# Neighbourhood attention: scores as one float32 product in four 64x64 tiles, 24 key columns per query half, bias tables from the host, value products joined over halves

## The chip, the cores and the metric

The kernel runs on one core of one Trainium2 chip. The metric is the device time of one execution in microseconds (us); lower is better. A core has TensorE (PE; its weight loads are listed apart as PEld), VectorE (DVE), ScalarE (ACT), GpSimd (POOL) and SyncE (SP), which here issues nearly all DMAs. Each engine takes its instructions in the order in which the program gives them.

## The reference

One layer over 2048 tokens of width 1024, which form a grid of 32 rows by 64 columns:

```python
h = rmsnorm(x, g)                                  # x (1, 2048, 1024), g = norm_0
q, k, v, gate = jnp.split(h @ w_in, 4, axis=-1)    # w_in (1024, 4096); 16 heads of 64
# per head; query (r, c); keys in 8 rows from clip(r - 4, 0, 24), 16 columns from clip(c - 8, 0, 48)
s = (q . k) / 8 + rpb[head, key_row - r + 7, key_col - c + 15]
o = softmax(s over those 128 keys) @ v
x = x + (o * silu(gate)) @ w_out                   # w_out (1024, 1024)
out = rmsnorm(x, norm_f)
```

All is float32. The learned bias `rpb` has 15 x 31 numbers per head.

## The kernel before

**Projections.** In the first half of the span (`stage_one`, `stage_two`) TensorE makes most of q, k, v and the gate. A product of float32 precision is there three products of values rounded to fewer bits (`F32R`): high x high, high x low, low x high. ScalarE copies the high half of an operand, VectorE subtracts it from the whole to get the low half. Results go to DRAM by `give`: q as it is, the gate after tanh, k split once more into a high and a low half (`hi`, `lo`, lines 370 to 375), which are stored apart.

**Attention.** It runs over 32 steps, one per pair of heads `p` and block of 8 query rows `T`, in the order `order`: T = 0 for all 8 pairs, then T = 1 and 2 for each pair, then T = 3 for all. Block T sees 11, 15, 15 or 12 key rows (`KEY_ROWS`). The 64 grid columns fall into four blocks C of 16; a block's queries (8 rows x 16 columns = 128, ordered as two halves of 8 columns each) see 24, 32, 32 or 24 key columns (`KEY_COLS`).

- `scores` (line 1025): for each C and each of the two heads `s` three F32R products, q's high and low half (split per step by `split_q`, which also scales by 1/8) against k's. The heads lie on partitions 0 to 63 and 64 to 127, so a product takes 64 rows of the array and all 128 columns. VectorE then adds the table `EM` and takes the minimum of the negated sum (line 1046); ScalarE takes the exponential with its sum (1052).
- Tables: the bias of a pair is loaded as padded rows (`load_e`) and POOL adds a mask to it per column kind (`bias`, line 1004); for T = 3 the finished table is loaded in six pieces (`load_last`).
- `normalise` (1055): a reciprocal on VectorE, then a multiplication per tile on POOL; in the second call of a step ScalarE does two of the four.
- `turns` (1087): 44 transposes of 64 queries each by TensorE into six PSUM banks; ScalarE and VectorE copy these to `pta` (1097).
- `values` (1126): per C, for each strip of 8 key columns, one float32 product per head, over 128 queries where both halves see the strip and over 64 where one does: 28 products per step. The heads take the two halves of the array's columns. VectorE multiplies by the gate (1149), and the result goes to DRAM for the output projection.

**Order of the work.** The main loop (1441 to 1487) writes it out by hand. In cycle m, `begin` queues loads; `feed` issues what is left of the projections, then of the output projection, about 24 matmuls per cycle in cycles 1 to 24 and more after; `consume` and `split_rows` put weight and activation splits between; then come `turns(m - 1)`, the two `scores` of step m and the `values` of step m - 1. `store(key, lag, f)` and `due` put a load or store on SyncE when the clock, which counts issued matmuls, has passed the lag. There are 8 PSUM banks, handed round in turn to projections, transposes, scores and values.

Of the kernel before, what the change touches and what calls it, by code (L numbers as in the profile page):

```python
# [10 lines left out]
F32 = mybir.dt.float32  # L11
# [13 lines left out]
RPB_ROWS, RPB_W = 26, 32  # L25
# [9 lines left out]
KEY_COLS = [(0, 24), (8, 40), (24, 56), (40, 64)]  # L35
# [4 lines left out]
MASK_N = [[(u1 - u0) * (v1 - v0) for v0, v1 in TYPE_COLS] for u0, u1 in TYPE_ROWS]  # L40
MASK_ALL = sum(sum(n) for n in MASK_N[:2])
LAST_ALL = sum(MASK_N[2])
# [3 lines left out]
def mask_table():  # L46
    out = []
    for t, (u0, u1) in enumerate(TYPE_ROWS):
        T = (0, 1, 3)[t]
        for c, (v0, v1) in enumerate(TYPE_COLS):  # L50
            C = (0, 1, 3)[c]
            half, qr, col, strip, kr, kc = np.ogrid[:2, T * 8:T * 8 + 8, :8, :(v1 - v0) // 8, T * 8 + u0:T * 8 + u1, :8]
            qc = C * 16 + half * 8 + col
            kc = C * 16 + v0 + strip * 8 + kc
# [3 lines left out]
            out.append(np.where(ok, 0.0, NEG).astype(np.float32).reshape(128, -1))  # L58
    return np.concatenate(out, axis=1)


def strips(C):
    out = []
    for s in range(KEY_COLS[C][0] // 8, KEY_COLS[C][1] // 8):
        halves = [h for h in range(2) if abs(2 * C + h - s) <= 1]
        out.append((s, s - KEY_COLS[C][0] // 8, halves[0] * 64, len(halves) * 64))
    return out
# [3 lines left out]
def build(ctx, tc, x, xr, xt, wg, rpb, last, w_out, n0, nf, masks, out):  # L71
# [4 lines left out]
    k_hi = [dram.tile([128, S], F32, name=f"k_hi{p}") for p in range(NP)]  # L76
    k_lo = [dram.tile([128, S], F32, name=f"k_lo{p}") for p in range(NP)]
# [12 lines left out]
    kp = pool("kp", 4)  # L90
# [14 lines left out]
    mp = pool("mp", 6)  # L105
# [41 lines left out]
    MK = []  # L147

    def load_masks():
        MK.append(mkp([128, MASK_ALL], BF16, "mk"))  # L150
        nc.sync.dma_start(MK[0], masks)


# [16 lines left out]
    def use_item(it):  # L170
# [6 lines left out]
        elif kind == "w":  # L177
# [12 lines left out]
            nc.scalar.activation(h, t, AF.Copy)  # L190
            nc.vector.tensor_tensor(l, t, h.bitcast(F32), OP.subtract)
# [102 lines left out]
    quiet = [False]  # L294

# [56 lines left out]
    def give(kind, hp, c, t, bank_=False):  # L352
# [11 lines left out]
        if kind == "q":  # L364
            if bank_:
                t = ev([128, 512], F32, "q")
                nc.scalar.activation(to(t), at, AF.Copy)
            store(("q", hp, c), 12, lambda: nc.sync.dma_start(qd[hp][:, s], t))
            return
# [39 lines left out]
    def seven_products(us, c0, X1, also):  # L409
# [11 lines left out]
        def form(n, P):  # L421
            src = A[n, uses[P][0]]
            F[n, P] = t = wp([128, 2, 512], F32R, "f")
            nc.scalar.activation(t[:, 0], src, AF.Copy)  # L424
            nc.vector.tensor_tensor(t[:, 1], src, t[:, 0].bitcast(F32), OP.subtract)  # L425
# [143 lines left out]
    def place_of(slot_):  # L569
        return slot_[0]([128, slot_[1]], F32R, "t")[:, :512] if isinstance(slot_, tuple) else slot_  # L570
# [6 lines left out]
    def stage_one():  # L577
        us = [("k", j) for j in range(4)] + [(k, j) for j in range(4) for k in "qg"]
        X1 = {f: [(xs([128, 512], F32R, "h"), xs([128, 512], F32R, "l")) for _ in range(4)]
              for f in ("B12", "B11", "B21", "B22")}  # L580
        spot = mkp([128, 3, 512], F32, "spot")
        land = {f: [p([128, n], F32, "land")[:, :512] for _ in range(4)]
                for f, p, n in (("x12", kp, 960), ("x22", xp, 512), ("x11", vh, 512))}
        sixth = sixths()
        land["x21"] = [spot[:, k] for k in range(3)] + [lp([128, 512], F32, "land")]
        slots = [(mp, 512)] * 6 + [(qp, 512)] * 2 + [(sp, 512)] * 2 + sixth[:2] + [(vh, 512)] * 4
        slots += sixth[2:] + [(kp, 960)] * 4
# [4 lines left out]
        def split(f, t, k, scale=None):  # L592
            if f == "T1":
                X1.setdefault(f, []).append((xs([128, 512], F32R, "h"), xs([128, 512], F32R, "l")))
            elif f[0] == "T":
                X1.setdefault(f, []).append((place_of(slots.pop(0)), place_of(slots.pop(0))))
# [4 lines left out]
        def load_rows(*hs):  # L601
            for t, j in hs:
                rows_in[t, j] = mp([128, 512], F32, "row")
                nc.sync.dma_start(rows_in[t, j], xr[t * 128:t * 128 + 128, 512 * j:512 * j + 512])

        def square_rows(*hs):
            for t, j in hs:
                square(t, j, rows_in.pop((t, j)))
# [192 lines left out]
    def stage_two():  # L801
# [3 lines left out]
        for k in range(4):  # L805
            load_x(2, "x22", k, x22[k])
        slots = {"T2": [(mp, 512)] * 4 + [(kp, 960)] * 4,
                 "T3": [(sp, 512)] * 2 + sixth[:5] + [(lp, 512)],
                 "T4": [(vh, 512)] * 4 + [(mp, 512)] * 2 + [sixth[5], (qp, 512)]}

        def also(n, i):
            if n == 0:
                if i == 0:
                    load_ahead()
                    load_e(0, 0, xp)[0]()
                elif i == 1:
                    load_e(0, 0, xp)[1]()
                    load_masks()
# [4 lines left out]
                if i in (4, 5):  # L823
                    bias(0, 0, i - 4)
                if i == 3:
                    for f in load_k(0, 0) + [load_q(0, 0)]:
                        f()
                if i == 5:
                    split_q(0, 0)
# [45 lines left out]
        def form(f, x, *ks):  # L875
            def g():
                for k in ks:
                    h, l = (place_of(a) for a in slots[f][2 * k:2 * k + 2])
# [55 lines left out]
    KT, VT, QT, EM, SG, E = {}, {}, {}, {}, {}, {}  # L934
# [9 lines left out]
    def width(C):  # L944
        return KEY_COLS[C][1] - KEY_COLS[C][0]

    def load_k(p, T):
        r0, r1 = KEY_ROWS[T]
        n = (r1 - r0) * GW
        must(*[("k", p, c) for c in range(r0 // 8, (r1 + 7) // 8)])  # L950
        KT[p, T] = []

        def keys(src):
            t = kp([128, 960], F32R, "kt")
            KT[p, T].append(t.rearrange("p (r c) -> p r c", c=GW))
            nc.sync.dma_start(t[:, :n].bitcast(F32), src[p][:, r0 * GW:r1 * GW])

        return [lambda: keys(k_hi), lambda: keys(k_lo)]

    def load_q(p, T):  # L960
        must(("q", p, T))

        def queries():
            QT[p, T] = t = lp([128, 512], F32, "qr")
# [3 lines left out]

    def split_q(p, T):
        t = QT[p, T]  # L970
        QT[p, T] = h, l = qp([128, 512], F32R, "qh"), qp([128, 512], F32R, "ql")
        split_to(h, l, t, HD ** -0.5)
# [13 lines left out]
    def load_e(p, ty, pool_=None):  # L986
        r0, r1 = (4, 15) if ty == 0 else (0, 15)

        def rows(s):
            t = (pool_ or ep)([128, 512], F32, "e")[:, :480]  # L990
            E[p, s] = t.rearrange("p (u v) -> p u v", v=32)
            nc.sync.dma_start(t[:, r0 * 32:r1 * 32], rpb[2 * p + s][:, r0 * 32:r1 * 32])

        return [lambda: rows(0), lambda: rows(1)]

    def bias(p, ty, cty):
        m0 = sum(sum(n) for n in MASK_N[:ty]) + sum(MASK_N[ty][:cty])
        (u0, u1), (v0, v1) = TYPE_ROWS[ty], TYPE_COLS[cty]
        n = MASK_N[ty][cty]
        sh = lambda a: a.rearrange("p (s u v) -> p s u v", u=u1 - u0, v=8)  # L1000
        for s in range(2):
            t = mp([128, 512], F32, "em")[:, :n]
# [537 lines left out]
```

## Time and profile before

| | |
|---|---|
| median of 3 runs | 1068.65 us (1068.24 to 1069.79) |
| span of the profiled execution | 1068.2 us, 0.4 below that median |
| busy: TensorE, VectorE, ScalarE, POOL | 1052.0, 739.8, 551.3, 261.9 us |
| score products, L1038 | 768 records, 550 to 999 us |
| value products, L1143 | 1792 records, 571 to 1013 us |
| transposes, L1121 | 1408 records, 566 to 1009 us |
| bias and mask on POOL, L1004 | 94 operations, 92.6 us |
| normalising on POOL and ScalarE, L1064 and L1062 | 192 and 64 operations |
| DMA | 206.53 MB |

A line of a group names the kernel's line, the engine and the operation, what is written and read, the shape, the count, the busy time and the mean length of one. Matmuls are pipelined: the length of one includes its way through the array, so the distance from start to start tells what it costs. In the order of time, records that follow each other and belong to one group are merged: start, length of the whole, count. A shape of 64\*128 means 64 rows and 128 columns of the array.

### The profile page before, as it was taken

The numbers are of one execution on the slowest core, as the hardware profiler recorded it, in microseconds if no ns is written. First come the engines' busy times: TensorE is split into PE (matmuls) and PEld (weight loads), VectorE is DVE, ScalarE is ACT, GpSimd is POOL, SyncE is SP. The second block draws the span as 40 slices with busy tenths as digits, with TensorE's granted clock in tenths as the row PEclk, the third lists the DMA queues.
The fourth block names the chain that finished last, engine by engine and source line by source line (L and its number), as shares of the span: only waits on it lengthen the run. The fifth ranks groups of instructions, "written<-read, shape, count | busy, mean of one in ns | idle before, by whom it ended". The sixth has DMA issues, their size and how long they took to land.

```text
span 1068.2 us, 20961 instructions
## 1 busy us (share of the span) xinstructions
PE 1052.0 (98%) x7596; PEld 876.8 (82%) x7596; DVE 739.8 (69%) x1608; ACT 551.3 (52%) x1285; POOL 261.9 (25%) x328
## 2 busy tenths in 40 slices
PE   9999999999999999999999999999998999999997
PEld 6888888887888888888888888888877888888886
DVE  5476888768897635566568677767777786667644
ACT  7645344333334334333347767778686765556422
POOL 0000322312311000000017775555445421212100
PEclk9999999999999999999999999999999999999999
DMA  9633665344645333524298789877986688787352
GB/s 320 212 99 108 197 205 178 124 134 140 176 129 150 116 89 92 173 90 169 85 317 265 230 244 302 266 237 237 295 271 214 209 285 294 223 262 252 105 158 79
DMA packets 129472, 206.53 MB, mean 193 GB/s; under 512 B 11800, under 2 KB 56088, under 8 KB 129368
## 3 DMA queue, kind: packets, MB, share of 16 engines
q1 hardware_dynamic: 128936, 204.79, 60.7%
q8 instruction: 60, 0.98, 0.4%
q14 instruction: 44, 0.36, 0.1%
q10 hardware_dynamic: 432, 0.40, 0.1%
HBM read 146.42 MB, written 58.72 MB: 192 GB/s over the span
## 4 chain that ended last, share of the span: by engine, by line
PE 86%; DVE 6%; DMA 2%; ACT 2%; issue 2%; POOL 1%; SPq 0%; DVEq 0%; ACTq 0%; POOLq 0%
PE pp L442 31%; PE pv L566 16%; PE s L1038 7%; PE o L1143 6%; PE po L1354 5%; PE po L1352 5%; PE po L1350 5%; PE ph L1121 3%; PE pp L390 3%; PE pp L388 3%; PE pp L386 3%; DVE x L1046 1%; DVE f L425 1%; DVE wol L196 1%; ACT x L1052 1%
## 5 line engine op out<-in xcount | busy, mean ns | idle before, releaser
L442 PE MATMUL pp<-h,f 128*128 128x512 f32 x608 | 196.7, 389 | 0.0
L1064 POOL TENSOR_SCALAR x<-x,st 128x480 f32<-128x480 f32 (+5 forms) x192 | 110.6, 593 | 261.9 <-DVE st L1057 240.4
L1052 ACT ACTIVATE x<-x,st 128x360 f32<-128x360 f32 (+5 forms) x256 | 151.2, 592 | 29.4 <-DVE st L1046 29.3
L1004 POOL TENSOR_TENSOR em<-e,mk 128x264 f32<-128x264 f32 (+3 forms) x94 | 92.6, 1019 | 211.1 <-DMA mk<-in_masks_dram 210.3
L442 PEld LDWEIGHTS pp<-h,f 128*128 128x128 f32 x608 | 114.1, 188 | 23.7
L442 PE MATMUL pp<-t,f 128*128 128x512 f32 x506 | 128.5, 390 | 0.3
L462 POOL TENSOR_TENSOR tmp<-tmp,rb 128x512 f32<-128x512 f32 x36 | 58.6, 1630 | 269.7 <-DVE tmp L460 210.3
L1046 DVE CUSTOM_DVE_ANT_0 x<-s,em 128x360 f32<-128x360 f32 (+5 forms) x256 | 123.4, 536 | 1.0 <-PE s L1038 1.0
L442 PE MATMUL pp<-l,f 128*128 128x512 f32 x304 | 118.3, 389 | 0.0
L442 PEld LDWEIGHTS pp<-t,f 128*128 128x128 f32 x506 | 94.8, 188 | 20.8 <-DVE u L455 1.1
L1354 PE MATMUL po<-wol,gh 128*128 128x512 f32 x252 | 99.3, 394 | 0.0
L1352 PE MATMUL po<-woh,gl 128*128 128x512 f32 x252 | 98.9, 392 | 0.3 <-DVE gl L1208 0.3
L1350 PE MATMUL po<-woh,gh 128*128 128x512 f32 x252 | 98.4, 391 | 0.0
L1038 PE MATMUL s<-kt,qh 64*128 64x480 f32 (+5 forms) x512 | 86.0, 382 | 7.6 <-issue 2.3
L566 PE MATMUL pv<-wh,h 128*128 128x512 f32 x256 | 88.8, 392 | 0.5 <-ACT h L527 0.5
L425 DVE TENSOR_TENSOR f<-raw,f 128x512 fp32r<-128x512 f32 x95 | 73.2, 771 | 22.4 <-ACT f L424 22.4
L566 PE MATMUL pv<-wl,h 128*128 128x512 f32 x256 | 88.6, 391 | 0.0
L566 PE MATMUL pv<-wh,l 128*128 128x512 f32 x256 | 88.3, 390 | 0.0
L1143 PEld LDWEIGHTS o<-pta,vt 120*64 120x64 f32 (+2 forms) x1792 | 81.9, 138 | 7.6 <-DVE st L1046 5.0
L1143 PE MATMUL o<-pta,vt 120*64 120x128 f32 (+5 forms) x1792 | 86.3, 254 | 0.0
L1097 DVE COPY pta<-ph 120x512 f32<-120x512 f32 (+5 forms) x96 | 57.2, 638 | 31.4 <-PE ph L1121 31.3
L1038 PEld LDWEIGHTS s<-kt,qh 64*128 64x128 f32 x512 | 62.1, 192 | 15.8 <-ACT pta L1097 3.9
(160 smaller groups left out, 1937.8 us busy)
## 6 DMA issues: line engine op xcount, KB each, us to landing
raw<-in_wg_dram SPq DMA_DIRECT2D x124, 256.0 KB, 4.9
row<-in_xr_dram SPq DMA_DIRECT2D x32, 256.0 KB, 3.9
vd<-v SPq DMA_DIRECT2D x32, 256.0 KB, 2.6
k_hi<-hi SPq DMA_DIRECT2D x32, 256.0 KB, 2.9
k_lo<-lo SPq DMA_DIRECT2D x32, 256.0 KB, 2.8
sgd<-sg SPq DMA_DIRECT2D x32, 256.0 KB, 2.9
qr<-qd SPq DMA_DIRECT2D x32, 256.0 KB, 3.9
sgt<-sgd SPq DMA_DIRECT2D x32, 256.0 KB, 7.0
```

The costliest lines, as they stand in the source:

```text
L425: nc.vector.tensor_tensor(t[:, 1], src, t[:, 0].bitcast(F32), OP.subtract)
L442: nc.tensor.matmul(B[n, P], t[:, int(m == 2), c], x[k][int(m == 1)], start=P in (1, 6, 5) and k == 0 and m == 0, stop=k == 3 and m == 2, s ...
L566: nc.tensor.matmul(ps[t], a[:, o], b, start=k == 0 and m == 0, stop=k == NK - 1 and m == 2)
L1004: (nc.gpsimd if attending[0] or not s else nc.vector).tensor_tensor(sh(t), E[p, s][:, u0 + 4:u1 + 4, v0 + 8:v1 + 8].rearrange("p u (s v) - ...
L1038: nc.tensor.matmul(pst[s], qq[a, qs], kk[a, :r1 - r0, c0:c1].rearrange("p r (s c) -> p s r c", c=8), start=(m == 0), stop=(m == 2))
L1046: nc.vector.tensor_tensor_reduce(X[i, C][s], pst[s], EM[p, ROW_TYPE[T], COL_TYPE[C], s], -1.0, 1e38, OP.add, OP.min, st[:, o:o + 1])
L1052: nc.scalar.activation(X[i, C][s], X[i, C][s], AF.Exp, bias=st[:, o:o + 1], scale=-1.0, accum_out=st[:, 4 + o:5 + o])
L1064: nc.gpsimd.tensor_scalar(X[i, C][s], X[i, C][s], st[:, o:o + 1], 1.0, op0=OP.mult, op1=OP.mult)
L1143: nc.tensor.matmul(to.rearrange("d (h q) -> d h q", q=64) if nq > 64 else to, vt[:k, strip, s * 64:s * 64 + 64], t[:k, h, at:at + 64] if n ...
L1350: nc.tensor.matmul(p, gh, woh[q, j], start=(i == 0), stop=False)
L1352: nc.tensor.matmul(p, gl, woh[q, j], start=False, stop=False)
L1354: nc.tensor.matmul(p, gh, wol[q, j], start=False, stop=(i == NK - 1))
```

## The change

- k is stored whole (`kd`) and loaded with 8 grid columns of margin on each side (`EDGE`); where there is none, POOL fills zeros. q is stored scaled: the 1/8 is in the split of q's weights. Both splits per step are gone.
- Scores: every query half of 8 columns sees 24 key columns from 8 to its left. Per C, half `h` and head `s` there is one float32 product, 64 rows by 64 columns of the array: four per C, where there were six F32R products.
- Tables: the host lays out bias and mask per pair, row kind, column kind and head, in the scores' order; one load per pair and row kind (128 x 1584, 2160 or 1728 numbers) brings six tables. POOL's additions and the mask are gone.
- `normalise` is all on POOL.
- `turns` goes strip place by strip place (j = 0, 1, 2), two banks each, and copies after each; the copies spread the blocks of 64 columns so that the queries that see one strip lie at a fixed distance.
- `values`: one product per strip and head over all halves that see it, 128 or 192 queries: 16 products per step.
- Buffers: k two tiles for four, tables two tiles of 2160 numbers for six of 512; the early stages use the new pools in their place.

```diff
-TYPE_ROWS = [(0, 11), (-4, 11), (-4, 8)]
-TYPE_COLS = [(0, 24), (-8, 24), (-8, 16)]
+TYPE_N = [(KEY_ROWS[t][1] - KEY_ROWS[t][0]) * 24 for t in (0, 1, 3)]
+TAB_AT = [6 * sum(TYPE_N[:t]) for t in range(4)]
+EDGE = 8
...
+def bias_tables(rpb):
...
+            kc = C * 16 + half * 8 + (strip - 1) * 8 + kc
...
+            tab = np.where(ok[None], rpb[:, dr, dc], np.float32(NEG)).reshape(NP, 2, 128, -1)
+            out += [tab[:, 0], tab[:, 1]]
+    return np.concatenate(out, axis=2)
...
-            nc.scalar.activation(h, t, AF.Copy)
-            nc.vector.tensor_tensor(l, t, h.bitcast(F32), OP.subtract)
+            split_to(h, l, t, HD ** -0.5 if KINDS["q"] <= u < KINDS["k"] else None)
...
-        hi = ev([128, 512], F32R, "hi")
-        lo = ev([128, 512], F32R, "lo")
-        nc.scalar.activation(to(hi), at, AF.Copy)
-        nc.vector.tensor_tensor(to(lo), at, to(hi.bitcast(F32)), OP.subtract)
-        store(("k", hp, c), 12, lambda: (nc.sync.dma_start(k_hi[hp][:, s], hi.bitcast(F32)),
-                                         nc.sync.dma_start(k_lo[hp][:, s], lo.bitcast(F32))))
+        if bank_:
+            t = ev([128, 512], F32, kind)
+            nc.scalar.activation(to(t), at, AF.Copy)
+        store((kind, hp, c), 12, lambda: nc.sync.dma_start((qd if kind == "q" else kd)[hp][:, s], t))
...
+            KT[p, T] = t = kp([128, 1024], F32, "kt")
+            n0, n1 = max(r0 * GW - EDGE, 0), min(r1 * GW + EDGE, S)
+            a = EDGE - (r0 * GW - n0)
+            if r0 == 0:
+                nc.gpsimd.memset(t[:, :a], 0.0)
+            if r1 == ROWS:
+                nc.gpsimd.memset(t[:, a + n1 - n0:a + n1 - n0 + EDGE], 0.0)
+            nc.sync.dma_start(t[:, a:a + n1 - n0], kd[p][:, n0:n1])
...
+    def load_tab(p, ty):
+        def table():
+            n = TYPE_N[ty]
+            t = emp([128, 2160], F32, "em")[:, :6 * n]
+            for c in range(6):
+                EM[p, ty, c // 2, c % 2] = t[:, c * n:c * n + n]
+            nc.sync.dma_start(t, tab[p, :, TAB_AT[ty]:TAB_AT[ty] + 6 * n])
...
-            for m, (qq, kk) in enumerate(((qh, kh), (qh, kl), (ql, kh))):
+            for h in range(2):
+                at = EDGE + (2 * C + h - 1) * 8
                 for s in range(2):
                     a = slice(s * 64, s * 64 + 64)
-                    nc.tensor.matmul(pst[s], qq[a, qs], kk[a, :r1 - r0, c0:c1].rearrange("p r (s c) -> p s r c", c=8), start=(m == 0), stop=(m == 2))
+                    keys = kt[a, at:at + r * GW].rearrange("p (r c) -> p r c", c=GW)[:, :, :24]
+                    nc.tensor.matmul(pst[s][h * 64:h * 64 + 64], qt[a, C * 128 + h * 64:C * 128 + h * 64 + 64],
+                                     keys.rearrange("p r (s c) -> p s r c", c=8), start=True, stop=True)
...
-                if both and j:
-                    nc.scalar.activation(X[i, C][s], X[i, C][s], AF.Copy, scale=st[:, o:o + 1])
-                else:
-                    nc.gpsimd.tensor_scalar(X[i, C][s], X[i, C][s], st[:, o:o + 1], 1.0, op0=OP.mult, op1=OP.mult)
+                nc.gpsimd.tensor_scalar(X[i, C][s], X[i, C][s], st[:, o:o + 1], 1.0, op0=OP.mult, op1=OP.mult)
...
+        for j in range(3):
+            b = [bank(512, f"ph{h}") for h in range(2)]
...
+                            nc.tensor.transpose(at[h][:k, s, C], X[2 * m + C // 2, C][s][q, j * k:j * k + k], ident[q, q])
             for h in range(2):
+                c = slice(cs[h][0], cs[h][-1] + 1)
                 (nc.vector.tensor_copy if h else lambda o, i_: nc.scalar.activation(o, i_, AF.Copy))(
+                    to[:k, :, 2 - j, c, h], at[h][:k, :, c])
...
+        for strip in range(8):
+            g0, g1 = max(strip - 1, 0), min(strip + 1, 7)
+            b = 9 * g0 + 8 * (1 - strip)
+            for s in range(2):
+                nc.tensor.matmul(o[s * 64:s * 64 + 64, g0 * 64:g1 * 64 + 64].rearrange("d (g q) -> d g q", q=64),
+                                 vt[:k, strip, s * 64:s * 64 + 64], t[:k, s, b:b + 9 * (g1 - g0) + 1:9],
+                                 start=strip == 0, stop=strip == 7, skip_group_check=True)
...
         if m + 1 < cycles:
-            nx = order[m + 1]
-            if nx[1] == 3:
-                later_loads(load_last(nx[0]), 12, 1.5)
-            later_loads(load_k(*nx), 14 if nx[1] < 3 else 22, 5)
+            p, T = order[m + 1]
+            if (p, ROW_TYPE[T], 0, 0) not in EM:
+                later_loads([load_tab(p, ROW_TYPE[T])], 12, 0)
+            later_loads([load_k(p, T)], 14, 0)
...
     def middle(m):
-        if 1 <= m < cycles:
-            split_q(*order[m])
...
-            values(2 * m - 2)
-            values(2 * m - 1)
+            values(m - 1)
```

More of the change, by code (lines that the diff above doesn't have):

```diff
@@ L567, in values_of, with fours, places_of @@
                     due(1)
[L569 to L570 removed]
+    def fours(p, n, dt):
+        t = p([128, n * 512], dt, "four")
+        return [t[:, i * 512:i * 512 + 512] for i in range(n)]
+    def places_of(slots):
+        for a in slots:
+            yield from fours(*a, F32R) if isinstance(a, tuple) else [a]
     X2 = {}
@@ L1403, in all_loads @@
             later.pop(0)[2]()
-    def next_sums(m):
-        return next((n for n in range(m + 1, cycles) if order[n][1] < 2), None)
     def begin(m):
         all_loads()
-        quiet[0] = False
         if m >= 1:
```

312 lines of the change are left out of this document (71 added, 241 removed).

## The prediction

> **What bounds the kernel now.** I read the page's chain of waits first, then TensorE's order of time in one cycle, then the stretches in which a cycle took longer than its neighbours.
>
> ```profile
> span 1068.2 us, 20961 instructions
> PE 1052.0 (98%) x7596; PEld 876.8 (82%) x7596; DVE 739.8 (69%) x1608; ACT 551.3 (52%) x1285; POOL 261.9 (25%) x328
> ...
> PE 86%; DVE 6%; DMA 2%; ACT 2%; issue 2%; POOL 1%; SPq 0%; DVEq 0%; ACTq 0%; POOLq 0%
> ```
>
> TensorE holds the chain, so an edit is worth what it takes from TensorE's own line: shorter blocks or fewer gaps. One undisturbed cycle of a middle row block (15 key rows), TensorE alone in order of time (start, length, instructions):
>
> ```profile
> 714.86 1.51 PE L1121 MATMUL ph<-ident,x 64*120 64x64 f32 x44
> 716.17 0.68 PE L1038 MATMUL s<-kt,qh 64*128 64x360 f32 x4
> 716.62 0.42 PE L1038 MATMUL s<-kt,ql 64*128 64x360 f32 x2
> 716.79 0.87 PE L1038 MATMUL s<-kt,qh 64*128 64x480 f32 x4
> 717.29 0.63 PE L1038 MATMUL s<-kt,ql 64*128 64x480 f32 x2
> 717.53 0.86 PE L1038 MATMUL s<-kt,qh 64*128 64x480 f32 x4
> ...
> 719.13 2.67 PE L1143 MATMUL o<-pta,vt 120*64 120x128 f32 x56
> 721.73 0.50 PE L390 MATMUL pp<-h,w 128*128 128x512 f32 x1
> 722.07 0.39 PE L386 MATMUL pp<-h,w 128*128 128x512 f32 x1
> ...
> 727.08 0.39 PE L388 MATMUL pp<-l,w 128*128 128x512 f32 x1
> 727.40 0.27 PE L1121 MATMUL ph<-ident,x 64*120 64x64 f32 x2
> ```
>
> From start to start: transposes 1.31 us, scores 2.96, values 2.60, projections 5.67; transposes to projections is 6.87. Between 722.07 and 727.08 stand 22 starts, 0.228 us for 512 columns: 0.445 ns per column and pass. The scores and values of this part are all that the change alters on TensorE. The score block of the first row block (11 key rows) and of the last (12):
>
> ```profile
> 616.74 0.60 PE L1038 MATMUL s<-kt,qh 64*128 64x264 f32 x4
> ...
> 619.12 2.67 PE L1143 MATMUL o<-pta,vt 88*64 88x128 f32 x56
> ...
> 884.47 0.64 PE L1038 MATMUL s<-kt,qh 64*128 64x288 f32 x4
> ...
> 886.98 2.67 PE L1143 MATMUL o<-pta,vt 96*64 96x128 f32 x56
> ```
>
> They take 2.38 and 2.51 us. There are 8 cycles of the first kind, 16 of the middle, 8 of the last.
>
> **Scores, the term that decides.** Today a column block of a head pair costs 3 products per head on a 64x128 part of the array, two heads side by side: from 716.79 to 717.53, 0.74 us for three 480-column slots, 0.247 each, 0.033 over the 0.214 that 480 columns cost at the projections' rate. So the two row halves do run together (one after the other, six would need 1.28 us). Afterwards there are 4 float32 products per block, each 64x64, and all have 24 columns per key row: 264, 360 or 288. What a float32 product costs is in the value block:
>
> ```profile
> L1143 PE MATMUL o<-pta,vt 120*64 120x128 f32 x512 | 39.8, 281 | 0.0
> L1143 PE MATMUL o<-pta,vt 120*64 120x64 f32 x384 | 22.2, 223 | 0.0
> ```
>
> The kernel issues 28 value products per cycle, 448 in the 16 middle cycles; the trace has 896 records. So one float32 product is two records, and 64 more columns cost 58 ns, 0.91 ns per column: each record is two passes at the projections' 0.445. Singly, a value block would need (32 x 128 + 24 x 64) x 0.89 = 5.0 us; it takes 2.60. Two column halves work together there, at 28 slots and 0.003 us over per slot ((2.60 - 2.51) / 28).
>
> Hence, if all four tiles work together, a tile does 4 blocks x 2 records = 8 slots per cycle of 360 x 0.89 = 0.320 us (264: 0.235; 288: 0.256). The tail: the present block of 2.96 less six slots of 0.247 and six of 0.193 (360 columns plus the same 0.033) leaves 0.32, which stays. Transposes and scores now share the 64-row layout; afterwards the array is cut anew between them, which I price by the first projection after the values, 0.34 us to the next start against 0.228: 0.11. So 2.56 + 0.02 + 0.32 + 0.11 = 3.01 against 2.96 in the middle cycles (+0.05), 2.33 against 2.38 (-0.05), 2.50 against 2.51 (-0.01): over 16, 8 and 8 cycles +0.3 us. Bounds: if each slot pays the scores' present 0.033 it is 8 x 0.03 x 32 = 7.7 us more, +8; if neither the new cut nor half of the tail is paid, (0.11 + 0.16) x 32 = 8.6 less, -8. I take 0, since the value records are the same kind of record with the same 64-column weights.
>
> Whether four tiles overlap is not in the trace. What is in it: how the records of the value block start.
>
> ```profile
> 668.13 0.33 PE L1143 MATMUL o<-pta,vt 120*64 120x128 f32 x2
> ```
>
> This is all of the value block up to 668.27: two records begin with the block and run side by side. The two records of one product use the same tile and are issued in succession, so the second to start must be the other head's, started past a record that waits. A queue per tile does that, and it would serve four tiles as well as two.
>
> The Trainium skill, "TensorE: Matmul & The Clock Gate" (Part 3, The mechanism), says otherwise: matmuls begin and end strictly in program order. By that rule the second half of each product would hold up the next tile and never more than two of the four would work: the slower rival below. "TensorEngine Tiling (Array Packing)" (Key Properties) says that tiles operate independently; the row at 668.13 agrees with this and not with the former.
>
> **Values.** The same columns (24 records of 192 and 8 of 128 are 5632, as are 32 of 128 and 24 of 64) in 16 slots for 28: 12 x 0.003 = 0.04 us, -1 us over 32 cycles; bounds 0 and -0.09 x 32 = -3.
>
> **Gaps.** Some cycles ran long. Columns: stretch, length, PE, PEld, DVE, ACT, POOL busy, granted TensorE clock, DMA:
>
> ```profile
> 752.40:758.90 6.50, 4.94 (x71) 3.98 (x70) 6.50 (x13) 2.82 (x8) 4.66 (x4) 0.90 0.93 261
> 758.90:762.50 3.60, 3.60 (x59) 3.53 (x57) 2.52 (x11) 3.60 (x12) 1.84 (x4) 0.70 0.91 365
> 807.70:811.20 3.50, 1.51 (x45) 1.36 (x44) 3.50 (x4) 0.01 (x1) 3.50 (x3) 1.00 0.79 265
> 811.20:816.50 5.30, 4.47 (x26) 3.96 (x26) 4.35 (x12) 4.37 (x12) 0.91 (x2) 0.68 0.94 338
> 849.80:858.20 8.40, 7.40 (x125) 6.29 (x124) 8.26 (x27) 5.38 (x16) 0.30 (x1) 1.00 0.88 292
> 863.90:871.40 7.50, 7.01 (x125) 6.03 (x124) 7.34 (x24) 5.27 (x16) 0.47 (x1) 1.00 0.98 320
> 794.10:802.00 7.90, 7.45 (x125) 6.25 (x125) 7.64 (x23) 6.05 (x18) 0.97 (x2) 1.00 0.88 302
> 676.30:684.10 7.80, 7.07 (x126) 6.22 (x125) 7.80 (x22) 5.15 (x15) 4.67 (x5) 1.00 0.91 315
> ```
>
> Each is one cycle's transposes, scores and values (the first two rows together; the 807.7 pair lacks a 2.60 value block). Against 6.87: 3.2, 4.5, 1.5, 1.0 and 0.9, and for 863.9, a last-row cycle (at most 1.31 + 2.51 + 2.60 = 6.42), 1.1: 12.2 us. VectorE is busy throughout, and a long gap costs twice, for the clock granted after it falls to 0.70 and 0.68. Why VectorE is late:
>
> ```profile
> 804.82 7.28 POOL L1004 TENSOR_TENSOR em<-e,mk 128x360 f32<-128x360 f32 x6
> 806.18 4.37 DVE L196 TENSOR_TENSOR wol<-raw,woh 128x512 fp32r<-128x512 f32 x3
> ...
> 811.08 1.27 DVE L1097 COPY pta<-ph 120x512 f32<-120x512 f32 x2
> ...
> 794.00 1.29 DVE L196 TENSOR_TENSOR wol<-raw,woh 128x512 fp32r<-128x512 f32 x2
> ```
>
> While POOL adds bias and mask, a VectorE subtraction takes 1.46 us; with POOL idle, 0.65. The copies out of the transposes' banks, due at 808, come at 811. The three cycles with over 3 us of POOL (676, 752, 807) hold 8.6 us. The change deletes these POOL additions (94), all VectorE and ScalarE work of splitting k (32 each; a k still in its bank keeps one ScalarE copy) and q (32 each), and shortens half of the score reads from 480 to 360 columns. I take 90% of the 8.6 and 60% of the other 3.6: -10 us; bounds -12 and, if other work fills VectorE, -3.
>
> **Edits at nothing.** ScalarE's two normalisations per pass go to POOL, which then does four in a row behind the second reciprocal:
>
> ```profile
> 723.11 0.18 DVE L1057 RECIPROCAL st<-st 128x4 f32<-128x4 f32 x1 [0.57 <-ACT x L1052]
> ...
> L1064 POOL TENSOR_SCALAR x<-x,st 128x360 f32<-128x360 f32 x32 | 17.8, 568 | 98.7 <-DVE st L1057 98.7
> ...
> kt<-k_hi SPq DMA_DIRECT2D x16, 480.0 KB, 6.3
> ```
>
> 723.3 + 4 x 0.57 = 725.6, and the transposes that wait start at 727.40: 1.8 us of cover, no more. The tables come as one load of 0.8 to 1.1 MB per head pair and row kind, on SyncE 12 matmuls into the projections of the cycle before their use: about 721.73 + 2.7 for a first score read at 741 (one cycle of 12.54 later than 728.7), 16 us ahead. A 480 KB load lands in 6.3 us; in proportion the largest table takes 14.5, an upper estimate, and is just covered. Behind it on SyncE and on the DMA queues stand the next k and q loads, which the scores need at the same time; k's low half (a store and a load) and the bias loads leave that queue, in the middle and last row blocks more bytes than the table adds, in the first row block 0.1 MB less per cycle. The scale in q's weight splits falls on ScalarE and VectorE six products ahead of use. POOL's 8-column fills beside k (one per head pair in the first and in the last row block) stand behind its normalising; each costs at most the 0.57 of a 360-column operation, with most of a cycle to spare. The transposes stay 44 per cycle, the copies from their banks 6 of the same total width. None of this reaches TensorE.
>
> **Sum.** 0 - 1 - 10 = -11 on the profiled 1068.2, and 0.4 for the median of the runs over that span: 1057.6. As the scores' lower bound is a rate rather than a mishap, I put the forecast a little lower, at 1057, with 1047 to 1066 as its own range.
>
> **Rivals.**
> A, slower: only two of the four tiles work at a time, in the score block, because a product's second record holds the next tile. 16 slots: 16 x 0.320 + 0.43 = 5.55 in the middle cycles (+2.6), 4.19 (+1.8), 4.53 (+2.0): 72 us, less the 11: 1129. For it: no row shows four. Against it: the start at 668.13. It decides once a slot is longer by 11 / 256 = 0.043 us.
> B, no change: VectorE stays late for other reasons and the slots pay the 0.033: 1068.6 + 8 - 1 - 3 = 1073; with only one of the two, 1065 or 1066. For it: 3.6 us of gaps have little POOL in them.
> C, POOL's normalising becomes the wait: if its operations took twice 0.57, the last would end 0.5 us after 727.4, in some 24 dense cycles 12 us, which cancels the gain: 1069. For it: POOL spans beside a busy VectorE; against it: 1.8 us of cover and an emptier POOL.
>
> **Chances.** Forecast 0.66, A 0.16, B 0.11, C 0.05, others 0.02. A measurement of this kernel tells about 0.2% from no change. Faster by more: the forecast and the better part of B, 0.69; within: 0.07; slower: A and the rest of B and C, 0.24. The range 1046 to 1080 leaves out A and the edges.
>
> **What would show it.** Score blocks in the new trace near 3.0, 2.3 and 2.5 us with records four deep: right; near 5.5: A. The stretches with 0.7 of the clock gone, and no VectorE subtraction at 1.46 us: the gaps' term is right. Transposes waiting for POOL: C. A score block under 2.8 us would mean that I priced its tail or rate too high.

## The result, and the profile after

| | before | after |
|---|---|---|
| median of the runs on one chip | 1069.22 us (1068.24 to 1070.02, 4 runs) | 1050.10 us (1049.85 to 1051.67, 4 runs) |
| ratio, 95% interval | | 0.9826 (0.9812 to 0.984) |
| span of the profiled execution | 1068.2 us | 1048.3 us |

The change is faster by 1.7%, 19 us; the forecast was 1057 us, with 1046 to 1080 as its range. The page after: span, busy time and the chain of waits.

```profile
span 1048.3 us, 19498 instructions
PE 1040.0 (99%) x7084; PEld 831.7 (79%) x7084; DVE 667.6 (64%) x1542; ACT 475.5 (45%) x1164; POOL 215.9 (21%) x314
...
PE 95%; DVE 1%; issue 1%; POOL 1%; ACT 1%; DMA 0%; SPq 0%; POOLq 0%; DVEq 0%; ACTq 0%
```

TensorE held 86% of the chain and now holds 95%; VectorE's share went from 6% to 1%. So two things went: some of TensorE's own work, and its gaps. The busy time (12 us less) doesn't tell the two apart, since a record that runs at a lower clock counts as busy for longer. The order of time of one undisturbed middle cycle, TensorE alone (start, length, instructions; transposes are L1017, scores L978, values L1035):

```profile
710.40 1.50 PE L1017 MATMUL ph<-ident,x 64*120 64x64 f32 x44
711.83 2.65 PE L978 MATMUL s<-kt,qt 64*64 64x360 f32 x32
714.41 2.61 PE L1035 MATMUL o<-pta,vt 120*64 120x128 f32 x32
...
722.63 1.50 PE L1017 MATMUL ph<-ident,x 64*120 64x64 f32 x44
```

From start to start the transposes take 1.43 us (1.31 before), the scores 2.58 (2.96). The same score blocks in the first and in the last row block:

```profile
603.61 2.25 PE L978 MATMUL s<-kt,qt 64*64 64x264 f32 x32
605.79 0.60 PE L1035 MATMUL o<-pta,vt 88*64 88x128 f32 x6
...
902.72 2.33 PE L978 MATMUL s<-kt,qt 64*64 64x288 f32 x32
904.99 0.60 PE L1035 MATMUL o<-pta,vt 96*64 96x128 f32 x6
```

2.18 and 2.27 us, where it was 2.38 and 2.51. Taken over all 32 cycles, as the medians of the distances between first starts:

| us, median | before: transposes, scores, values | after |
|---|---|---|
| first row block (8 cycles) | 1.240, 2.397, 2.595 | 1.358, 2.184, 2.538 |
| middle (16) | 1.311, 2.962, 2.595 | 1.427, 2.581, 2.538 |
| last (8) | 1.241, 2.516, 2.595 | 1.363, 2.263, 2.537 |

Scores: 8 x 0.213 + 16 x 0.381 + 8 x 0.253 = 9.8 us less; transposes about 0.12 each, 3.8 us more; values 0.057 each, 1.8 us less: 7.8 us. What single cycles take above the median of their row block (called excess below) was 13.5 us in all and is 1.5: 12.0 us. Together 19.8, and the spans differ by 19.9.

### The profile page after: what moved, and what is told of

It reads as the page before. It is cut to its first block, busy times and chain, and to the rows that moved or that the text cites. A ratio compares the mean times of both kernels' runs of the same rounds, so it can differ in the third digit from the quotient of the medians.

```text
span 1048.3 us, 19498 instructions
## 1 busy us (share of the span) xinstructions
PE 1040.0 (99%) x7084; PEld 831.7 (79%) x7084; DVE 667.6 (64%) x1542; ACT 475.5 (45%) x1164; POOL 215.9 (21%) x314
## 4 chain that ended last, share of the span: by engine, by line
PE 95%; DVE 1%; issue 1%; POOL 1%; ACT 1%; DMA 0%; SPq 0%; POOLq 0%; DVEq 0%; ACTq 0%
PE pp L415 33%; PE pv L539 16%; PE o L1035 8%; PE s L978 7%; PE po L1244 5%; PE po L1242 5%; PE po L1240 5%; PE ph L1017 4%; PE pp L364 4%; PE pp L362 4%; PE pp L360 3%; POOL x L1001 1%; DMA raw<-in_wg_dram 0%; DVE f L501 0%; ACT x L992 0%
## 5 line engine op out<-in xcount | busy, mean ns | idle before, releaser
L1001 POOL TENSOR_SCALAR x<-x,st 128x360 f32<-128x360 f32 (+2 forms) x256 | 155.1, 625 | 297.4 <-DVE st L997 256.9
L992 ACT ACTIVATE x<-x,st 128x360 f32<-128x360 f32 (+2 forms) x256 | 139.8, 548 | 27.3 <-DVE st L986 27.3
L415 PE MATMUL pp<-four,f 128*128 128x512 f32 x520 | 131.2, 390 | 0.1
L415 PEld LDWEIGHTS pp<-four,f 128*128 128x128 f32 x520 | 97.5, 188 | 21.3 <-DVE u L428 0.5
L986 DVE CUSTOM_DVE_ANT_0 x<-s,em 128x360 f32<-128x360 f32 (+2 forms) x256 | 108.7, 479 | 2.0 <-PE s L978 2.0
L1035 PEld LDWEIGHTS o<-pta,vt 120*64 120x64 f32 (+2 forms) x1024 | 68.5, 137 | 22.8 <-DVE st L986 15.2
L1035 PE MATMUL o<-pta,vt 120*64 120x192 f32 (+5 forms) x1024 | 83.4, 316 | 0.0
L978 PE MATMUL s<-kt,qt 64*64 64x360 f32 (+2 forms) x1024 | 80.0, 436 | 0.0
L1020 ACT ACTIVATE pta<-ph 120x512 f32<-120x512 f32 (+5 forms) x96 | 46.8, 556 | 54.0 <-PE ph L1017 54.0
L415 PEld LDWEIGHTS pp<-l,f 128*128 128x128 f32 x304 | 57.0, 188 | 12.1
L364 PE MATMUL pp<-h,w 128*128 128x512 f32 x160 | 64.2, 401 | 0.0
```

What stands on the lines that cost most here:

```text
L364: nc.tensor.matmul(p, wl[w, b][:, cols], hh[k, c], start=False, stop=(k == NK - 1))
L415: nc.tensor.matmul(B[n, P], t[:, int(m == 2), c], x[k][int(m == 1)], start=P in (1, 6, 5) and k == 0 and m == 0, stop=k == 3 and m == 2, s ...
L978: nc.tensor.matmul(pst[s][h * 64:h * 64 + 64], qt[a, C * 128 + h * 64:C * 128 + h * 64 + 64], keys.rearrange("p r (s c) -> p s r c", c=8), ...
L986: nc.vector.tensor_tensor_reduce(X[i, C][s], pst[s], EM[p, ROW_TYPE[T], COL_TYPE[C], s], -1.0, 1e38, OP.add, OP.min, st[:, o:o + 1])
L992: nc.scalar.activation(X[i, C][s], X[i, C][s], AF.Exp, bias=st[:, o:o + 1], scale=-1.0, accum_out=st[:, 4 + o:5 + o])
L1001: nc.gpsimd.tensor_scalar(X[i, C][s], X[i, C][s], st[:, o:o + 1], 1.0, op0=OP.mult, op1=OP.mult)
```

## The experiments

Ratios are set against the kernel before on the same chip (medians of 1069.8, 1069.1 and 1069.8 us for the three groups of runs).

### The tables alone

The kernel before, with finished tables loaded for every row kind; the scores, the splits and the normalising stay as they were.

```diff
-            if nx[1] == 3:
-                later_loads(load_last(nx[0]), 12, 1.5)
+            if (nx[0], ROW_TYPE[nx[1]], 0, 0) not in EM:
+                later_loads(load_last(nx[0], ROW_TYPE[nx[1]]), 12, 1.5)
...
-        if (p, ty, 0, 0) not in EM:
-            for cty in range(3):
-                bias(p, ty, cty)
```

> The kernel before with one part of the change alone: all bias tables come finished from the host (six loads per head pair and row kind, as it already does for the last row block), POOL's additions are gone; F32R scores over 24 and 32 columns, k and q splits, normalising and values as before. Theory (POOL's additions slow VectorE, and that makes the three long gaps, 8.6 us by the trace): 1058 to 1062 us. Rival (the gaps went because VectorE and ScalarE lost the splits): 1066 to 1070 us.

1061.03 us (1059.98 to 1061.74), ratio 0.9913 (0.9887 to 0.9939). VectorE's weight splits, by line, in the kernel before:

```profile
L191 DVE TENSOR_TENSOR w<-raw,w 128x512 fp32r<-128x512 f32 x20 | 21.9, 1119 | 1.5 <-ACT w L190 1.5
...
L196 DVE TENSOR_TENSOR wol<-raw,woh 128x512 fp32r<-128x512 f32 x16 | 15.1, 994 | 0.0
```

and in this one:

```profile
L191 DVE TENSOR_TENSOR w<-raw,w 128x512 fp32r<-128x512 f32 x20 | 13.1, 685 | 1.3 <-ACT w L190 1.3
L196 DVE TENSOR_TENSOR wol<-raw,woh 128x512 fp32r<-128x512 f32 x16 | 10.1, 686 | 0.0
```

On average 1119 and 994 ns become 685 and 686, since no split meets an addition any more. The blocks' medians are unchanged, the excess falls from 13.5 to 4.2 us, and the stretches that held the two long gaps (columns: stretch, length, PE, PEld, DVE, ACT, POOL busy, clock, DMA) now keep TensorE busy throughout, at full clock:

```profile
749.00:760.00 11.00, 11.00 (x143) 9.62 (x142) 8.62 (x25) 8.85 (x24) 3.22 (x6) 1.00 1.05 364
800.00:806.40 6.40, 6.40 (x77) 5.44 (x77) 6.07 (x13) 4.27 (x11) 0.00 (x0) 1.00 0.85 243
806.00:812.00 6.00, 6.00 (x77) 5.27 (x75) 4.15 (x15) 5.75 (x19) 3.37 (x6) 1.00 0.79 299
```

So the additions are needed for the long gaps. Whether they are enough is the next question.

### The additions put back

The changed kernel, with six additions per table on POOL again, into a scratch tile that nothing reads.

```diff
+        for c in range(6):
+            nc.gpsimd.tensor_tensor(SCR[0][:, c % 3 * 512:c % 3 * 512 + n].rearrange("p (s u v) -> p s u v", s=3, v=8),
+                                    sh(EM[p, ty, c // 2, c % 2]), sh(EM[p, ty, c // 2, 1 - c % 2]), OP.add)
...
+                if k == 2 and m < cycles:
+                    added(m)
```

> The changed kernel with 84 additions on POOL put back at their old place (six per head pair and row kind but the last, 264 or 360 columns, two table pieces into a scratch tile that nothing reads). Theory: VectorE is slowed again and gaps return: 1054 to 1059 us. Rival: 1050 to 1052 us, since VectorE has lost enough work to stay ahead.

1049.91 us (1049.49 to 1051.68), ratio 0.9814 (0.9792 to 0.9837): nothing comes back, though the trace has 74.6 us of additions (90 of them, where I had counted 84). The order of time on VectorE and POOL in one such cycle says why:

```profile
790.01 6.42 POOL L1001 TENSOR_SCALAR x<-x,st 128x360 f32<-128x360 f32 x8 [5.79 <-DVE st L997]
...
792.50 3.03 DVE L180 TENSOR_TENSOR wol<-raw,woh 128x512 fp32r<-128x512 f32 x4 [0.34 <-ACT woh L179]
...
796.39 5.53 POOL L1324 TENSOR_TENSOR scr<-em 128x360 f32<-128x360 f32 x6
```

POOL now has eight normalisations to do before the additions, and VectorE's splits (0.76 us each) are over at 795.5, before the first addition. The theory as I had written it for this run, that additions on POOL slow VectorE wherever they stand, is refuted. What the rows of the kernel before had shown was narrower, additions at the same moment as splits, and this run didn't put that back: the theory of coincidence was untested.

### The additions and q's split

The same, and q's high and low half made per step again (one ScalarE copy, one VectorE operation).

```diff
+        if 1 <= m < cycles:
+            split_to(ep([128, 512], F32R, "qh"), ep([128, 512], F32R, "ql"), QT[order[m]], HD ** -0.5)
```

> The same with POOL's additions and also the q split of each step put back (one ScalarE copy and one VectorE operation of 512 columns per step, into scratch tiles that nothing reads). Theory: most of the 12 us of gaps is back, 1057 to 1063 us, of which the additions make at least two thirds. Rival: the split alone makes them, so 4 us or more above the run with the additions alone.

1052.37 us (1052.24 to 1054.12), ratio 0.9838 (0.9816 to 0.986), excess 4.1 us. Neither expectation came: q's split costs 2.5 us over the run before, and the long gaps stay away. The weight splits still run beside the normalising, at a mean of 823 ns.

### ScalarE normalises again

The changed kernel with two of the four normalisations of a step's second call back on ScalarE.

```diff
+                if both and j:
+                    nc.scalar.activation(X[i, C][s], X[i, C][s], AF.Copy, scale=st[:, o:o + 1])
```

> The changed kernel, but ScalarE does two of the four normalisations of a step's second call again, as in the kernel before. If POOL's normalising is covered (the trace shows 1.9 us between its end and the transposes), the time stays: 1049.5 to 1050.5 us. If it held up the transposes anywhere, the transposes' waits for POOL (1.9 us in the whole span) go and the kernel is faster by at most that: 1048 us. ScalarE's later weight halves could cost up to 1 us.

1050.81 us (1050.17 to 1051.72), ratio 0.983 (0.9809 to 0.9851), excess 2.2 us: no gain. In the changed kernel the clean middle cycle has

```profile
716.21 4.52 POOL L1001 TENSOR_SCALAR x<-x,st 128x360 f32<-128x360 f32 x8 [7.74 <-DVE st L997]
718.17 0.18 DVE L997 RECIPROCAL st<-st 128x4 f32<-128x4 f32 x1 [0.42 <-ACT x L992]
```

so in this cycle POOL ends at 720.7 and the transposes start at 722.63: 1.9 us of cover. All waits of the transposes for POOL come to 1.9 us in five places, by the waits of TensorE's weight loads:

```profile
PEld ph L1017 <- POOL x L1001: 1.9, 5, 0.5
```

### The additions beside the splits

With ScalarE normalising as in the run before, POOL reaches its additions earlier and VectorE its splits later. Two runs put the additions on top of that, without and with q's split.

> The changed kernel with the additions on POOL of the earlier run (six per table, into a scratch tile), and ScalarE doing two of the four normalisations of a step's second call again. In the earlier run POOL came to its additions only after eight normalisations, when VectorE's weight splits were over: no split ran beside an addition, and the time stayed at 1049.9. Now they start about 1.2 us earlier and the splits come about 1.2 us later. If it is the coincidence of the two that slows VectorE, splits of over 1.2 us appear in the trace again, and the time is 1052 to 1058 us. If additions on POOL do no harm to VectorE, it stays at 1050.

> As the run before, and with the split of q per step as well (a copy on ScalarE, a subtraction on VectorE): nearly all the work beside TensorE that stood between the normalising and the next copies in the kernel before. By the theory that VectorE's lateness needs both, its own load and additions that coincide with it, the gaps come back: 1056 to 1062 us, with some 8 to 12 us of blocks over their medians. If the splits of k in the projections or the loads of the old tables made the gaps, they don't: 1052 to 1053 us, as in the earlier run with additions and q's split but without ScalarE's normalising.

1055.99 us (1054.75 to 1057.73), ratio 0.9878 (0.9857 to 0.9898), and 1062.90 us (1062.23 to 1063.68), ratio 0.9939 (0.9918 to 0.9959); excess 6.6 and 13.6 us. Against the run with the same normalising and no additions that is some 5 us for the additions alone, which cost nothing where they came after the splits, and some 12 us with q's split, which had cost 2.5 us where the additions came late. VectorE and POOL in one cycle of the second, in order of time:

```profile
800.27 7.79 POOL L1329 TENSOR_TENSOR scr<-em 128x360 f32<-128x360 f32 x6
...
801.71 5.55 DVE L180 TENSOR_TENSOR wol<-raw,woh 128x512 fp32r<-128x512 f32 x4
807.18 0.68 DVE L1133 TENSOR_TENSOR y<-po,xr 128x512 f32<-128x512 f32 x1
807.78 1.74 DVE L1023 COPY pta<-ph 120x512 f32<-120x512 f32 x3
```

The longest waits of its TensorE (total, times, longest):

```profile
PE s L978 <- DVE y L1133: 3.4, 2, 3.1
PE s L978 <- DVE pta L1023: 2.3, 1, 2.3
```

Its two stretches with the long gaps (columns as above):

```profile
748.70:755.50 6.80, 4.45 (x69) 2.78 (x72) 6.80 (x11) 2.23 (x6) 4.76 (x4) 0.83 0.83 274
755.50:759.40 3.90, 3.90 (x44) 2.38 (x36) 2.65 (x13) 3.90 (x14) 1.79 (x4) 0.86 0.91 321
803.30:812.40 9.10, 5.99 (x78) 3.49 (x77) 8.28 (x16) 3.78 (x10) 4.76 (x4) 0.81 0.63 214
```

A split takes 5.55 / 4 = 1.39 us here and an addition 1.30. The reads of the PSUM banks (`y` from the projection's, `pta` from the transposes') queue behind the splits on VectorE, the scores wait for them, and the granted clock falls to 0.81 to 0.86: the picture of the kernel before, made out of the changed kernel by additions whose result nobody reads. In the stretch from 755.50 TensorE isn't idle: the granted clock is 0.50 there until 756.6, and the score slots start 0.60 us apart, twice the 0.302 of an undisturbed cycle.

What is slowed is narrower than "VectorE". In the run without q's split, the weight splits and the additions as groups (for the additions: shortest, median and longest length):

```profile
L180 DVE TENSOR_TENSOR wol<-raw,woh 128x512 fp32r<-128x512 f32 x16 | 15.5, 1025 | 6.7 <-ACT woh L179 6.7
```

```profile
L1327 POOL TENSOR_TENSOR scr<-em x90: 743/961/1427, 560.1 to 827.3; 128x360 f32<-128x360 f32 x48, 128x264 f32<-128x264 f32 x42
```

The mean of 1025 ns is made of two kinds: the eight splits that lie at least half beside additions take 1364 on average, the eight that lie clear 686. The copies of PSUM banks (line 1023) take 655 beside and 632 clear. The additions suffer too: those beside the eight slow splits have 360 columns (the 743 is one of 264), and they take 1.41 us where a split lies beside them throughout and 0.96 clear of splits. The Trainium skill, "SBUF — State Buffer" (SBUF: two separate sides), says that VectorE and GpSimd share one pair of ports under an exclusive lock, which a VectorE operation takes against a reading GpSimd operation when both its inputs are in SBUF. The trace agrees in which operations suffer, and nearly in the size: a split and an addition side by side take about 1.4 us, where strict turns would take 0.69 + 0.96 = 1.65.

### Two tiles in place of four

Both heads' products on the first head's rows, which leaves the second head's scores out.

```diff
-                    a = slice(s * 64, s * 64 + 64)
+                    a = slice(0, 64)
```

> The changed kernel, but the score products of both heads take q and k from the first head's 64 partitions, so that a block's four products use two tiles of the array (rows 0 to 63) instead of four. This leaves the second head's scores out. If the four tiles of the changed kernel work together, a cycle now needs 16 slots instead of 8: 8 x 0.302 us more in the 16 middle cycles, 8 x 0.222 and 8 x 0.243 in the 8 first and 8 last ones, 68 us together: 1112 to 1120 us, with score blocks near 5.0, 4.0 and 4.2 us. If only two tiles had worked at a time in the changed kernel (the slower rival of the prediction), nothing changes: 1050 us.

1115.18 us (one execution). The score block of a middle cycle:

```profile
707.12 5.11 PE L978 MATMUL s<-kt,qt 64*64 64x360 f32 x32
712.15 2.61 PE L1035 MATMUL o<-pta,vt 120*64 120x128 f32 x32
```

5.04 us, 2.46 more: the eight slots that rival A wanted, at 0.307 each. In the changed kernel all four tiles work at once. Its own trace shows it directly; this is all that lies before 711.9 of the block that starts at 711.83:

```profile
711.83 0.53 PE L978 MATMUL s<-kt,qt 64*64 64x360 f32 x4
```

The four start within 0.02 us, the next four 0.353 us after the first, then four more every 0.302.

### Head by head

The same products in another order: per call all four of one head, then all four of the other.

```diff
-            for h in range(2):
...
-                for s in range(2):
+            got.append((C, [bank(n, f"s{s}") for s in range(2)]))
+        for s in range(2):
+            for C, pst in got:
+                for h in range(2):
```

> The changed kernel, but the score products of a call go head by head: all four of head 0 (two per tile, in two tiles), then all four of head 1; the products are the same. If each tile has a queue that takes at least two products (three records waiting behind the one that runs), head 1's tiles start at once and nothing changes: 1050 us, score blocks 2.58. If a tile keeps no more than one product, the second product of head 0 holds head 1 back by one product: two slots more per cycle, 0.60 us in the middle cycles, 0.44 and 0.49 in the others, 17 us: 1066 to 1069 us, score blocks near 3.2 us.

1051.87 us (one execution); score blocks 2.63 us. All that lies before 713.0 of the block that starts at 712.92:

```profile
712.92 0.57 PE L979 MATMUL s<-kt,qt 64*64 64x360 f32 x4
```

Four tiles again, though four products of head 0 stand ahead of head 1's first, two for each of its tiles. Head 1's tiles start 0.05 us behind, not a product's 0.60. So at least the rest of one product and a whole second one can wait on a tile while a later product starts on another. The Trainium skill's rule that the prediction named, "TensorE: Matmul & The Clock Gate" (Part 3, The mechanism), has matmuls begin and end in program order. The starts of this run go against it: by that rule head 1 could not start before head 0's second products, 0.60 us behind. A hold of one product would have cost some 17 us, as expected beforehand; the run took 1.8 us more than the change.

### Whole tiles for the scores

Float32 products as in the change, but 64x128 over all 128 queries of a column block, with 24 or 32 key columns as before; VectorE goes on to read the first 24 of them, so the second halves get the wrong keys.

```diff
-            for h in range(2):
-                at = EDGE + (2 * C + h - 1) * 8
...
+            c0, c1 = ((0, 24), (8, 40), (24, 56), (40, 64))[C]
...
+                keys = kt[a, at:at + r * GW].rearrange("p (r c) -> p r c", c=GW)[:, :, :c1 - c0]
+                nc.tensor.matmul(pst[s], qt[a, C * 128:C * 128 + 128],
+                                 keys.rearrange("p r (s c) -> p s r c", c=8), start=True, stop=True)
```

> The changed kernel with float32 scores on 64x128 of the array: one product per column block and head over 24 or 32 key columns, for all 128 queries. VectorE still reads 24 strips' worth, the first three strips, so the second query halves get the wrong keys; all other work is unchanged. Theory (a slot costs its columns times two passes, whatever the tile, and the cut between transposes and scores costs 0.12 us): 8 slots of 0.30 and 0.40 in the middle cycles, score block 2.98 against 2.58 us, transposes 1.31 against 1.43, in all 7 to 8 us more, 1057 to 1058 us. Rival (128-column weight loads aren't hidden in the 64-row layout, 0.033 us per slot as in the kernel before): 1065 us.

1057.97 us (one execution). The score block of a middle cycle:

```profile
702.86 3.04 PE L978 MATMUL s<-kt,qt 64*128 64x360 f32 x16
705.83 2.61 PE L1036 MATMUL o<-pta,vt 120*64 120x128 f32 x32
```

2.97 us: the same eight slots, four of them with 480 columns. The slots are 0.302 us apart for 360 columns and 0.402 for 480, 0.42 ns per column and pass in both, as in the change. So a slot costs its columns, whatever the tile's width, and the smaller tiles bring only the 8 key columns that a half doesn't see: 4 x 0.10 = 0.40 us. They cost 0.09: the transposes take 1.337 here from start to start against 1.427. The tile of the scores behind them is all that differs there, so I read the 0.09 as the price of cutting the array anew.

The run shows one thing more: float32 products in whole tiles take as long as the kernel before with its three F32R products (2.97 against 2.96 us). In the score block itself the exchange of three products for one gained nothing; only the smaller tiles with their fewer columns did. A 480-column slot of the kernel before took 0.247 us where 480 x 0.42 would be 0.202; no run shows where the 0.045 came from.

### Value products per half

```diff
-            for s in range(2):
...
-                                 vt[:k, strip, s * 64:s * 64 + 64], t[:k, s, b:b + 9 * (g1 - g0) + 1:9],
...
+            for g in range(g0, g1 + 1):
+                for s in range(2):
+                    nc.tensor.matmul(o[s * 64:s * 64 + 64, g * 64:g * 64 + 64],
+                                     vt[:k, strip, s * 64:s * 64 + 64], t[:k, s, b + 9 * (g - g0)],
+                                     start=strip == 0 and g == 0, stop=strip == 7, skip_group_check=True)
```

> The changed kernel, but each value product takes the queries of one half only: 44 products of 64 queries per step instead of 16 of 128 or 192, the same columns in all. By the prediction's 0.003 us per slot, 28 slots more cost 0.08 us in each of 32 cycles, 2.7 us: 1053 us; by what the join of the change brought (0.057 us for 12 slots, 0.005 each), 4.3 us: 1054 us, value blocks 2.67 us. If the weight loads, now 88 per step, can't keep up with passes of 64 columns, the block is longer: 1060 us or more, value blocks near 3 us.

1055.87 us (1055.42 to 1057.46), ratio 0.9879 (0.9853 to 0.9905).

```profile
705.06 2.79 PE L1036 MATMUL o<-pta,vt 120*64 120x64 f32 x88
```

The block is 2.715 us from start to start against 2.538: 0.177 for 28 slots, 0.0063 each, 5.7 us over 32 cycles. The price of a slot is small but twice what I took.

## Why the prediction was right

The direction, the mechanism and the range held; the time came out 7 us under the forecast. Six of the 19.8 us came from the scores, the term that I had put at nothing, so the forecast's direction rested on the gaps. By the prediction's own steps, on the profiled span:

| term | predicted | measured |
|---|---|---|
| scores, with the array's cut | 0 (-8 to +8) | -6.0 (scores -9.8, the cut in the transposes +3.8) |
| values | -1 (-3 to 0) | -1.8 |
| gaps | -10 (-12 to -3) | -12.0 |
| sum | -11 | -19.8 |

**Scores: right mechanism, mis-sized term.** The step that was off is "2.56 + 0.02 + 0.32 + 0.11 = 3.01": measured 2.58. Of the 0.43, 0.14 is the slot, 0.302 and not 0.320: I had taken the rate from the distance of the projections' starts, 0.228 for 512 columns, as if it were all columns; at the measured 0.42 ns, 0.013 of it belongs to the start of a record. 0.02 is the slot's overhead, which four tiles don't show. 0.16 is the tail: the block has 0.16 us over eight slots, not 0.32. The 0.32 was not a tail alone. At the end of the same old block the two heads' tiles are out of step (their last records are the two of `ql`):

```profile
718.65 0.34 PE L1038 MATMUL s<-kt,ql 64*128 64x360 f32 x1
718.67 0.34 PE L1038 MATMUL s<-kt,qh 64*128 64x360 f32 x1
718.85 0.35 PE L1038 MATMUL s<-kt,ql 64*128 64x360 f32 x1
719.13 2.67 PE L1143 MATMUL o<-pta,vt 120*64 120x128 f32 x56
```

One tile starts its last record 0.20 us behind the other; in the change the last four start within 0.02 us, and without such a lag the old remainder would have been about 0.14. 0.11 is the cut, which the change pays, but before the scores' first start, in the transposes' interval (+0.12, of which the whole-tile run shows 0.09 as the cut). The prediction's test "under 2.8 us would mean that I priced its tail or rate too high" names it. In the first and last row blocks the block is 2.18 and 2.26 us, more than 8 x 0.222 + 0.16 = 1.94 and 8 x 0.242 + 0.16 = 2.10: there three of the four records of the fifth slot start 0.1 to 0.2 us late. In the first row block shown, the last VectorE copy out of the transposes' banks ends 1.08 us after the scores begin, and the trace names it as what the next weight load waits for. No run tests this.

**Values.** 0.057 us per cycle for 12 slots where I had 0.04; within its bounds, and the run with halves apart gives the same kind of price.

**Gaps.** The step "three cycles with over 3 us of POOL hold 8.6 us" is borne out by the tables alone: the excess falls by 9.3 us and the run by 8.7. The other 3.6 us I had put at 60%; of the 4.2 left there, 2.7 go with the other parts of the change. The condition was narrower than I had it: POOL's additions don't slow VectorE, they slow its operations with both inputs in SBUF, and only when the two run at the same time. With the additions after the splits nothing is lost, with them beside the splits, and q's split on VectorE besides, as much as in the kernel before (13.6 us of excess). The signs named for the gaps came: no VectorE subtraction of the attention part takes over 1.03 us, the output weights' splits take 0.81 us on average where they took 0.99, and the two cycles that still ran longest (0.9 and 0.7 us over) have the full clock:

```profile
783.80:791.26 7.46, 7.12 (x109) 5.24 (x109) 6.78 (x22) 5.63 (x18) 1.67 (x3) 1.00 0.98 371
833.67:840.87 7.20, 7.20 (x109) 4.75 (x109) 6.97 (x23) 5.55 (x17) 0.67 (x2) 1.00 0.72 273
```

```profile
L180 DVE TENSOR_TENSOR wol<-raw,woh 128x512 fp32r<-128x512 f32 x16 | 12.2, 813 | 1.4 <-ACT woh L179 1.0 <-DMA sgt<-sgd 0.3
```

What is left in these two cycles isn't the old cause. In the second, the scores wait for VectorE's copies behind its work for the output. In the first, the transposes wait for the normalising:

```profile
781.71 3.01 POOL L1001 TENSOR_SCALAR x<-x,st 128x360 f32<-128x360 f32 x2
782.79 1.57 DVE L180 TENSOR_TENSOR wol<-raw,woh 128x512 fp32r<-128x512 f32 x2
...
784.77 1.21 PE L1017 MATMUL ph<-ident,x 64*120 64x64 f32 x32 [0.34 <-POOL x L1001]
```

**Edits at nothing.** TensorE waits 1.9 us in all for the normalising on POOL, and the run that undoes it is not faster. The table load

```profile
em<-in_tab_dram SPq DMA_DIRECT2D x8, 1080.0 KB, 7.9
```

lands in 7.9 us; the upper estimate of 14.5, in proportion to a smaller load (6.3 x 1080 / 480 gives 14.2), was nearly double, and 16 us of lead were ample.

**Rivals.** A (two of four tiles) is out: the run with two tiles costs 65 us more than the change. B needed late VectorE work and dearer slots; neither came. C (POOL becomes the wait) got its condition and not its price: 22 of the 256 normalisations, all of them beside VectorE operations with both inputs in SBUF, take 1.43 to 1.52 us in place of 0.48 to 0.57. But at most three of them fall in a cycle, the cover takes most of it up, and the waits come to 1.9 us, not 12.

## What to carry to other kernels

Where small products fill only a part of the array, count slots by the columns of the longest tile: four 64x64 tiles gave here what two 64x128 did, and the gain was in the columns that needn't be computed. To find what a GpSimd operation costs, see which VectorE operations run beside it and where their inputs lie; moving it to another moment in the cycle was worth as much as deleting it. And take a rate from two sizes of the same kind of record, not from one.

## What was not expected of the hardware

- Products of different tiles pass one another: with two products per tile ahead in program order, the other head's tiles still started 0.05 us after the first.
- A float32 slot of the scores costs 0.42 ns per column and pass (0.302 us for 360 columns, 0.402 for 480) and nothing beside it, with two tiles or four at work.
- The cut of the array between the transposes and 64x64 products cost 0.09 us.
- A VectorE subtraction of two SBUF operands took 1.36 us beside POOL's additions and 0.69 clear of them; copies from PSUM took 0.66 and 0.63. Beside the normalising it is POOL that loses: a normalisation that met splits took 1.5 us (3.01 for 2) where one in the clean cycle took 0.57 (4.52 for 8), while the splits took 0.81 on average.
